# Attention-stage stores issued from GpSimd's queue, and a three-buffer ring for streamed weights

## The chip, the cores and the metric

The kernel runs on one core of one Trainium2 chip. The core has five engines that follow separate instruction streams: TensorE (PE in the profile, with its weight loads as PEld), VectorE (DVE), ScalarE (ACT), GpSimd (POOL) and SyncE (SP), which here only issues DMA transfers. Data lives in SBUF (on-chip, 128 partitions), matmul results in PSUM, everything else in HBM. The metric is device time in microseconds of one execution. The kernel before took 1733.87 us (median of three runs, 1732.55 to 1734.95).

## The reference, cut to what matters

One decoder block on 1024 tokens of width 1024, in float32. A normalised input `h` is projected by one wide weight; the parts are queries, keys and values of 24 heads in three groups (dilation 1, 4 and 16, window of 128 steps each), a gated convolution branch, and two gates. The three groups of a head slot are merged with their softmax denominators as weights.

```python
h = rms_norm(x, g_pre_mix)
q, k, v, glu_in, z_ga, z_gc = split(h @ w_in)
for g, (window, dilation) in enumerate(((128, 1), (512, 4), (2048, 16))):
    o_g, lse_g = dilated_group_attention(q[g], k[g], v[g], bias_tab[g], window, dilation)
alpha = softmax(stack(lses))                      # over the three groups
y_attn = sum_g(alpha[g] * outs[g]) @ w_attn_out
y_conv = silu(layer_norm(depthwise_conv31(u * sigmoid(gate)))) @ w_conv_out + b
merged = sigmoid(z_ga) * y_attn + sigmoid(z_gc) * y_conv
x = x + rms_norm(merged @ w_mix_out, g_post_mix)
x = x + rms_norm(swiglu(rms_norm(x, g_pre_ffn)), g_post_ffn)
```

## The kernel before, in words

Every large product is made from values split in two float32r parts, a high one and the rest, so one product is three matmuls (L321 to L323, or L305 to L309, or L940 to L944 for the values). The order of all work is written out by hand in one Python program; each engine executes its instructions in that order, and an instruction waits for the data and for the buffer that it needs.

**Buffers.** Most tiles are 128x1024 float32 and come from one pool, `slot()`, tag "b", of NSLOT = 43. `ring()`, tag "d", has NRING = 2 of the same size; it holds the attention outputs `O` of groups 0 and 1 and the residual rows `x2` of the mixing stage. `half()`, tag "c", has 11 of 128x512. A new tile takes the buffer that was released longest ago, and its first writer waits for the last user of that buffer.

**Stages, in order of time.** (1) The start and the plain projections, to about 111 us. (2) Twenty-three *pairs* to about 550 us: two weight tiles, "row1" and "row2", make one 2x2 block product in the manner of Winograd, seven products of 12 matmuls (`winograd`, `prod`). For the next pair SP loads the two raw tiles (`load_ahead`, L177), ACT makes the high parts (L195, L231), GpSimd the rest (L196, L232) and the sums of quarters: `s12` (L215, L216) and `s34` (L222, L223), in `quarters`. ACT also copies PSUM results out (L335, L340, L345). Beside it VectorE computes the convolution (L684). (3) Values and attention, to about 875 us. `v()` computes the values of one group for four heads at a time, six calls; each call writes two 128x1024 tiles `x`, ACT copies the results in (L950, L952), and `out` stores each by two transfers (L927). `timed()` fixes when, within a call, the weights of the next call are loaded and split: 6 and 15 ticks after its start (a tick is six matmuls there). Between these matmuls runs `attention()`: 96 steps in 12 stacks of 8, a stack being one group and one pair of heads. A step takes scores (L1038, `att_s`), adds the bias tile (L1041, DVE; the tile is loaded at L477), exponentiates (L1051, ACT), transposes (L1074, ACT L1079 and DVE L1080 take the parts) and multiplies with the values (L1095, L1097), of which VectorE makes the output (L1102). Before a stack, SP loads its operands (L866, L867, L873) and its values (L903 to L908), and GpSimd splits the values (L917, `value_parts`) and copies query parts across partitions (L882, L883, `double`; eight casts per stack). At the end of a stack of group 0 or 1, `tokens_out` stores its statistics and its output (L1060 for group 0, one transfer; L1064 for group 1, two transfers). `merge` combines the groups of a pair of heads; for the first two pairs the result goes to HBM (L1165). (4) Gates, output projections, mixing, and the FFN, whose first product is again made of pairs (twenty), to 1727 us. VectorE, not GpSimd, makes the sums there.

**Queues.** All these stores and loads are issued by SP, in program order. A transfer that waits for its data, or for a buffer, holds all transfers behind it in that queue.

Of the kernel before, what the change touches and what calls it, by code (L numbers as in the profile page):

```python
# [43 lines left out]
PLAIN = 2  # L44

LAST = 5
NSLOT = 43

NRING = 2
NHALF = 11  # L50


# [6 lines left out]
def f(ap):  # L59
    return ap.bitcast(F32)  # L60


class Build:
# [16 lines left out]
    def slot(self, dt=F32, shape=None):  # L80
        self.uid += 1
        return self.pool.tile(shape or [128, 1024], dt, tag="b", bufs=NSLOT, name=f"b{self.uid}")

    def ring(self):
        self.uid += 1
        return self.pool.tile([128, 1024], F32, tag="d", bufs=NRING, name=f"d{self.uid}")

# [84 lines left out]
    def load_ahead(self, i):  # L172
        while self.sent < min(len(self.jobs), i + 1):
            j = self.sent
            src, n, _ = self.jobs[j]
            self.raw[j] = self.slot()
            self.nc.sync.dma_start(self.raw[j][:, :n], src)  # L177
            self.sent += 1

# [19 lines left out]
    def quarters(self, i, c):  # L199


        nc = self.nc
        if c == 0:
            self.hl[i] = {}
        o = self.hl[i]
        r1, r2 = self.raw[i - 1], self.raw[i]
        a11, a12, a21, a22 = r1[:, :H], r1[:, H:], r2[:, :H], r2[:, H:]
        add = self.wsplit.tensor_tensor
        l, r = slice(0, H), slice(H, 2 * H)
        if c == 0:  # L210
            h, w = self.both(r1)
            o["A11"], o["A12"] = (h[:, l], w[:, l]), (h[:, r], w[:, r])
        elif c == 1:
            self.s12 = self.slot()
            add(self.s12[:, l], a21, a22, op=OP.add)  # L215
            add(self.s12[:, r], self.s12[:, l], a11, op=OP.add)  # L216
        elif c == 2:
            h, w = self.both(self.s12)
            o["S1"], o["S2"] = (h[:, l], w[:, l]), (h[:, r], w[:, r])
        elif c == 3:  # L220
            self.s34 = self.slot()
            add(self.s34[:, l], a11, a21, op=OP.add)  # L222
            add(self.s34[:, r], self.s12[:, r], a12, op=OP.add)  # L223
            self.s12 = None
        elif c == 4:
            h, w = self.both(self.s34)
            o["S3"], o["S4"] = (h[:, l], w[:, l]), (h[:, r], w[:, r])
            self.s34 = None
        else:
            x = self.slot(F32R)  # L230
            nc.scalar.copy(x[:, l], a22)  # L231
            add(x[:, r], a22, f(x[:, l]), op=OP.subtract)  # L232
            o["A22"] = (x[:, l], x[:, r])
            del self.raw[i], self.raw[i - 1], self.hl[i]
# [90 lines left out]

    def winograd(self, W, T, f11, f12, f21, f22):

# [5 lines left out]
        x1, x2, v1 = self.half(), self.half(), self.half()  # L333
        self.prod(X, W["A11"], T["B11"], True, False)
        nc.scalar.copy(x1, X)  # L335
        self.prod(Z, W["A12"], T["B21"], True, True)
        rest = f11(Z, x1)
        Z = x1 = None
        self.prod(X, W["S2"], T["T2"], False, False)
        nc.scalar.copy(x2, X)  # L340
        V = self.bank()
        if rest:
            rest()
        self.prod(V, W["S1"], T["T1"], True, False)
        nc.scalar.copy(v1, V)  # L345
        if self.sums:
            self.finish(self.sums)
            self.sums = None
            self.summed()
        self.prod(X, W["S3"], T["T3"], False, False)  # L350
        rest = f22(X, v1)
# [374 lines left out]
    def glu_pair(self, j, job):  # L726
# [12 lines left out]
        def f22(x, v):  # L739
            nc.vector.scalar_tensor_tensor(v, x, self.nbu[:, j:j + 1], v, op0=OP.add, op1=OP.add)  # L740
            s[1] = v
# [178 lines left out]
    def v(self, g, hg, now, then):  # L920

        nc = self.nc
        W = self.timed(now, then, 6, 15)

        def out(i, x):
            for e in range(2):
                nc.sync.dma_start(self.d_v[g, 2 * hg + e].rearrange("(t p) c -> p t c", p=128)[:, i - 2:i + 2],  # L927
                                  x.rearrange("p (t e c) -> p t e c", t=4, e=2)[:, :, e])
            self.vn += i == 6

        for i in range(0, 8, 2):
            ps = self.bank()
            for e in range(2):
                t = slice((i + e) * 128, (i + e + 1) * 128)
                o = ps[:, e * 256:(e + 1) * 256]
                for kt in range(KT):
                    hi, lo = W[kt // 4]
                    s = slice((kt % 4) * 256, (kt % 4 + 1) * 256)
                    a, b = self.hH[kt][:, t], self.hL[kt][:, t]
                    nc.tensor.matmul(o, a, hi[:, s], start=kt == 0, stop=False)  # L940
                    self.beat()
                    nc.tensor.matmul(o, a, lo[:, s], start=False, stop=False)  # L942
                    self.beat()
                    nc.tensor.matmul(o, b, hi[:, s], start=False, stop=kt == KT - 1)  # L944
                    self.beat()
                    if kt % 2:
                        self.tick()
            if i % 4 == 0:
                x = self.slot()
                nc.scalar.copy(x[:, :H], ps)  # L950
            else:
                nc.scalar.copy(x[:, H:], ps)  # L952
                self.later(2, lambda i=i, x=x: out(i, x))
                x = None
# [101 lines left out]
    def tokens_out(self, g, dst, src):  # L1056

        if g == 0:
            d = dst.rearrange("(u p) e -> p u e", p=128)
            self.nc.sync.dma_start(d, src)  # L1060
        else:
            d = dst.rearrange("(b p c) e -> b p c e", b=2, c=4)
            for b in range(2):
                self.nc.sync.dma_start(d[b], src[:, b::2, :])  # L1064

    def att_t(self, a):

# [43 lines left out]
    def merge(self, hp, st, last):  # L1111


        nc = self.nc

        late = 1 + (hp > 1)
        while hp > 1 and (self.fine is not None or hp > len(self.OT) + 2):
            yield 0
        O = [*self.others(hp), last]
        last = None  # L1120
        yield 1 + late
        t = self.tiny(96, "mrg", 2)
        m, r = (t[:, i * 16:(i + 1) * 16].rearrange("p (u e) -> p u e", u=8) for i in range(2))
        w = t[:, 48:].rearrange("p (g u e) -> p g u e", g=3, u=8)
        low, tot = st[:, :, :, 0:2], st[:, :, :, 2:4]
        nc.vector.tensor_reduce(m, low.rearrange("p g u e -> p u e g"), AX.X, OP.min)
        nc.vector.tensor_tensor(w, low, m.unsqueeze(1).to_broadcast([128, 3, 8, 2]), op=OP.subtract)
        nc.scalar.activation(t[:, 48:], t[:, 48:], AF.Exp, scale=-1.0)
        yield late
        nc.vector.tensor_tensor(tot, tot, w, op=OP.mult)  # L1130
        nc.vector.tensor_reduce(m, tot.rearrange("p g u e -> p u e g"), AX.X, OP.add)
        nc.vector.reciprocal(r, m)
        nc.vector.tensor_tensor(w, w, r.unsqueeze(1).to_broadcast([128, 3, 8, 2]), op=OP.mult)
        for g in range(3):
            y = O[g].rearrange("p (u h c) -> p u h c", u=8, h=2)
            a = w[:, g].unsqueeze(3).to_broadcast([128, 8, 2, 64])
            nc.vector.tensor_tensor(y, y, a, op=OP.mult)
            yield late
        nc.vector.tensor_tensor(O[1], O[1], O[2], op=OP.add)
        O[2] = y = a = None  # L1140
        yield late
        nc.vector.tensor_tensor(O[0], O[0], O[1], op=OP.add)
        O[1] = None
        yield 2 + 2 * late
        if hp < 2:
            hi = self.slot()
        else:
            hi, lo = self.slot(F32R), self.slot(F32R)
        for h in range(2):
            ps = self.bank("t")  # L1150
            for i in range(4):
                u = h * 4 + i
                nc.tensor.transpose(ps[:, i * 128:(i + 1) * 128], O[0][:, u * 128:(u + 1) * 128], self.ident)
            y = ps.rearrange("p (u m) -> p u m", u=4)
            a = hi.rearrange("p (m u) -> p u m", u=8)[:, h * 4:h * 4 + 4]
            nc.scalar.copy(a, y)
            if hp > 1:
                nc.vector.tensor_tensor(lo.rearrange("p (m u) -> p u m", u=8)[:, h * 4:h * 4 + 4], y, f(a),
                                        op=OP.subtract)
            ps = y = a = None  # L1160
            yield late
        if hp > 1:
            self.OT[hp] = hi, lo
        else:
            self.nc.sync.dma_start(self.d_ot[hp], hi)  # L1165

    def out_parts(self):

# [790 lines left out]
```

## Time and profile before

| what | before |
|---|---|
| median of three runs | 1733.87 us |
| the profiled execution | 1728.74 us |
| its span, first to last instruction | 1726.9 us |
| PE busy | 1703.5 us, 99% |
| DVE, ACT, POOL busy | 1237.1, 793.7, 462.5 us |
| granted TensorE clock | 0.999 |
| stores that the change moves (L927, L1060, L1064, L1165) | 24 + 8 + 16 + 2 transfers |

The profiled execution lies 1.8 us above its span, and 5.1 us below the median. Lines of the profile name an instruction by its source line; `x<-y` is output from input by tile name, and what stands in brackets after an instruction, or after a bar, is the idle time of its engine before it and what ended that time. "SPq" is SP's issuing queue; "b", "c" and "d" are the three kinds of buffers.

### The profile page before, as it was taken

What the parts mean: (1) busy time and instruction counts of PE and PEld (TensorE: products, weight loads), DVE (VectorE), ACT (ScalarE), POOL (GpSimd) and SP (SyncE); (2) the same over time, 40 slices, a digit from 0 to 9 for tenths busy, and PEclk for the clock granted to TensorE, in tenths of its full rate; (3) what the DMA queues carried; (4) which work ended last, traced back from release to release, by engine and by line L of the source; (5) the groups of instructions that cost most, each with busy time, mean ns of one, the idle gap of its engine ahead of it and who ended that gap; (6) DMA issues with size and microseconds to landing.
All of it is one profiled execution on the core that took longest, in us unless ns stands there. A gap on an engine that the chain in (4) does not pass through costs nothing.

```text
span 1726.9 us, 24514 instructions
## 1 busy us (share of the span) xinstructions
PE 1703.5 (99%) x8698; PEld 1448.2 (84%) x8698; DVE 1237.1 (72%) x2217; ACT 793.7 (46%) x1552; POOL 462.5 (27%) x337
## 2 busy tenths in 40 slices
PE   8999999999999999999999999999999999999998
PEld 7778888887888999999788888888888888888886
DVE  6879988789998576687664855676556555677686
ACT  6344343434444486667622346643333333454453
POOL 0017777787786043443300120000000000000000
PEclk9999999999999999999999999999999999999999
DMA  4342344345667898988945732223322322395334
GB/s 164 125 160 86 110 160 133 135 159 184 206 164 194 246 257 200 245 227 213 310 145 187 275 107 93 83 73 112 126 92 92 112 108 92 137 363 159 107 126 153
DMA packets 185398, 277.03 MB, mean 160 GB/s; under 512 B 55185, under 2 KB 106892, under 8 KB 185276
## 3 DMA queue, kind: packets, MB, share of 16 engines
q1 hardware_dynamic: 184876, 274.97, 50.2%
q8 instruction: 68, 1.11, 0.3%
q14 instruction: 54, 0.44, 0.1%
q10 hardware_dynamic: 288, 0.27, 0.0%
q0 software_dynamic: 112, 0.24, 0.0%
HBM read 184.81 MB, written 95.33 MB: 162 GB/s over the span
## 4 chain that ended last, share of the span: by engine, by line
PE 86%; POOL 5%; DVE 3%; DMA 3%; ACT 2%; issue 2%; SPq 0%; DVEq 0%; POOLq 0%; ACTq 0%
PE p L321 13%; PE p L322 13%; PE p L323 13%; PE p L1843 12%; PE p L1572 5%; PE p L305 5%; PE p L307 5%; PE p L309 5%; PE p L942 2%; PE p L940 2%; PE p L944 2%; POOL b L196 2%; PE p L554 2%; PE p L1038 2%; PE p L1074 2%
## 5 line engine op out<-in xcount | busy, mean ns | idle before, releaser
L321 PE MATMUL p<-b,b 128*128 128x512 f32 x1204 | 469.4, 390 | 3.7 <-ACT c L335 2.4
L323 PE MATMUL p<-b,b 128*128 128x512 f32 x1204 | 468.8, 389 | 0.2 <-POOL b L196 0.2
L322 PE MATMUL p<-b,b 128*128 128x512 f32 x1204 | 468.5, 389 | 0.0
L321 PEld LDWEIGHTS p<-b,b 128*128 128x128 f32 x1204 | 226.0, 188 | 53.7 <-ACT c L335 3.2
L323 PEld LDWEIGHTS p<-b,b 128*128 128x128 f32 x1204 | 226.0, 188 | 48.5 <-POOL b L196 1.3
L322 PEld LDWEIGHTS p<-b,b 128*128 128x128 f32 x1204 | 226.0, 188 | 46.4
L195 ACT CAST b<-b 128x1024 fp32r<-128x1024 f32 x131 | 137.8, 1052 | 178.4 <-DVE b L216 50.9
L1843 PE MATMUL p<-b,b 128*128 128x512 f32 x924 | 209.6, 389 | 0.0
L1843 PEld LDWEIGHTS p<-b,b 128*128 128x128 f32 x924 | 173.4, 188 | 36.0
L196 POOL TENSOR_TENSOR b<-b,b 128x1024 fp32r<-128x1024 f32 x66 | 158.8, 2406 | 116.3 <-ACT b L195 108.1
L196 DVE TENSOR_TENSOR b<-b,b 128x1024 fp32r<-128x1024 f32 x65 | 79.5, 1222 | 128.9 <-ACT b L195 128.9
L684 DVE SCALAR_TENSOR_TENSOR p<-b,par,p 128x511 f32<-128x511 f32 (+14 forms) x232 | 163.4, 738 | 0.0
L305 PE MATMUL p<-b,b 128*128 128x512 f32 x368 | 147.6, 401 | 0.0
L309 PE MATMUL p<-b,b 128*128 128x512 f32 x368 | 146.2, 397 | 0.0
L307 PE MATMUL p<-b,b 128*128 128x512 f32 x368 | 146.1, 397 | 0.0
L940 PE MATMUL p<-b,b 128*128 128x256 f32 x384 | 115.3, 300 | 0.0
L942 PE MATMUL p<-b,b 128*128 128x256 f32 x384 | 114.6, 298 | 0.0
L944 PE MATMUL p<-b,b 128*128 128x256 f32 x384 | 114.5, 298 | 0.0
L1180 DVE TENSOR_TENSOR b<-c,b 128x512 fp32r<-128x512 f32 x101 | 69.9, 693 | 46.9 <-ACT b L1179 46.6
L1179 ACT CAST b<-c 128x512 fp32r<-128x512 f32 x101 | 62.4, 618 | 63.8 <-DMA c<-dqA 19.8
L1179 ACT CAST b<-b 128x512 fp32r<-128x512 f32 x117 | 72.4, 619 | 40.6 <-DVE b L387 13.7
L1180 DVE TENSOR_TENSOR b<-b,b 128x512 fp32r<-128x512 f32 x117 | 80.3, 690 | 14.8 <-ACT b L1179 13.1
(226 smaller groups left out, 2994.1 us busy)
## 6 DMA issues: line engine op xcount, KB each, us to landing
b<-w_in SPq DMA_DIRECT2D x53, 512.0 KB, 5.7
b<-w_fi SPq DMA_DIRECT2D x44, 512.0 KB, 4.9
dk<-c SPq DMA_DIRECT2D x48, 256.0 KB, 5.7
dq<-c SPq DMA_DIRECT2D x48, 256.0 KB, 4.3
b<-dq SPq DMA_DIRECT2D x48, 256.0 KB, 8.9
b<-dk SPq DMA_DIRECT2D x48, 256.0 KB, 7.3
dqS<-c SPq DMA_DIRECT2D x44, 256.0 KB, 2.1
b<-w_fo SPq DMA_DIRECT2D x44, 256.0 KB, 5.3
```

Of the source, the lines that this page charges most:

```text
L196: self.wsplit.tensor_tensor(lo, x, f(hi), op=OP.subtract)
L305: nc.tensor.matmul(ps, hi[:, s], a, start=kt == 0, stop=False)
L307: nc.tensor.matmul(ps, hi[:, s], b, start=False, stop=False)
L309: nc.tensor.matmul(ps, lo[:, s], a, start=False, stop=kt == nk - 1)
L321: nc.tensor.matmul(ps, hi[:, s], a, start=first and kt == 0, stop=False, skip_group_check=True)
L322: nc.tensor.matmul(ps, hi[:, s], b, start=False, stop=False, skip_group_check=True)
L323: nc.tensor.matmul(ps, lo[:, s], a, start=False, stop=kt == 3, skip_group_check=True)
L684: nc.vector.scalar_tensor_tensor(A[i][:, j:], src[i][:, :H - j], w[i], A[i][:, j:], op0=OP.mult, op1=OP.add)
L940: nc.tensor.matmul(o, a, hi[:, s], start=kt == 0, stop=False)
L942: nc.tensor.matmul(o, a, lo[:, s], start=False, stop=False)
L1180: nc.vector.tensor_tensor(s[:, 512:512 + n], src, f(s[:, :n]), op=OP.subtract)
L1843: nc.tensor.matmul(acc[t], x, y, start=first and e == 0, stop=last and e == 2, skip_group_check=True)
```

## The change

Four edits. The stores of the values, of the attention outputs, of the statistics and of the first two merged heads are issued by GpSimd's queue and not by SP's. The ring grows from two buffers to three and the pool shrinks from 43 to 42, so the number of large buffers is the same. The raw row1 tiles, `s12` and the value tiles `x` come from the ring and no longer from the pool. In `v()` the next weights are loaded at tick 4 (6 before) and queued for splitting at tick 16 (15 before).

```diff
-NSLOT = 43
-NRING = 2
+NSLOT = 42
+NRING = 3
@@ load_ahead
-            src, n, _ = self.jobs[j]
-            self.raw[j] = self.slot()
+            src, n, kind = self.jobs[j]
+            self.raw[j] = self.ring() if kind == "row1" else self.slot()
@@ quarters
-            self.s12 = self.slot()
+            self.s12 = self.ring()
@@ v
-        W = self.timed(now, then, 6, 15)
+        W = self.timed(now, then, 4, 16)
...
-                nc.sync.dma_start(self.d_v[g, 2 * hg + e]...
+                nc.gpsimd.dma_start(self.d_v[g, 2 * hg + e]...
...
-                x = self.slot()
+                x = self.ring()
@@ tokens_out
-            self.nc.sync.dma_start(d, src)
+            self.nc.gpsimd.dma_start(d, src)
...
-                self.nc.sync.dma_start(d[b], src[:, b::2, :])
+                self.nc.gpsimd.dma_start(d[b], src[:, b::2, :])
@@ merge
-            self.nc.sync.dma_start(self.d_ot[hp], hi)
+            self.nc.gpsimd.dma_start(self.d_ot[hp], hi)
```

More of the change, by code (lines that the diff above doesn't have):

```diff
@@ L922, in v @@
         nc = self.nc
-        W = self.timed(now, then, 6, 15)
+        W = self.timed(now, then, 4, 16)
         def out(i, x):
             for e in range(2):
-                nc.sync.dma_start(self.d_v[g, 2 * hg + e].rearrange("(t p) c -> p t c", p=128)[:, i - 2:i + 2],
+                nc.gpsimd.dma_start(self.d_v[g, 2 * hg + e].rearrange("(t p) c -> p t c", p=128)[:, i - 2:i + 2],
                                   x.rearrange("p (t e c) -> p t e c", t=4, e=2)[:, :, e])
```

## The prediction

> **What bounds the kernel now.** I read the page's first lines, then the waits of TensorE, then the busy times by stage, and only then the queues of SP and POOL around each stall. Matmuls fill the span; only 23.4 us of it are free, and of these the change can touch at most what lies between start and end.
>
> ```profile
> span 1726.9 us, 24514 instructions
> ...
> PE 1703.5 (99%) x8698; PEld 1448.2 (84%) x8698; DVE 1237.1 (72%) x2217; ACT 793.7 (46%) x1552; POOL 462.5 (27%) x337
> ```
>
> The waits of PE (engine, line, releaser: us in total, times, longest) say which idle time there is. The first row is the start, which no edit touches.
>
> ```profile
> PE p L554 <- ACT b L530: 6.0, 1, 6.0
> PE p L1097 <- DVE c L1080: 3.7, 5, 1.2
> PE p L321 <- ACT c L335: 2.4, 2, 2.0
> PE p L1038 <- DVE stat L1041: 1.3, 1, 1.3
> ```
>
> By stage (busy us of PE, PEld, DVE, ACT, POOL in brackets with counts, then clock, DMA share, GB/s): the early pairs are full, the later pairs lose a little, and the values and attention lose 4.9 us. The granted clock is 1.00 in all three, so nothing is to be had from it.
>
> ```profile
> 125.00:350.00 225.00, 225.00 (x995) 186.29 (x994) 197.60 (x285) 89.40 (x133) 174.80 (x101) 1.00 0.36 120
> 350.00:550.00 200.00, 198.52 (x866) 161.64 (x865) 178.32 (x234) 84.53 (x126) 158.01 (x89) 1.00 0.61 180
> 572.00:847.00 275.00, 270.15 (x2252) 265.05 (x2251) 193.95 (x591) 184.08 (x532) 99.67 (x118) 1.00 0.88 233
> ```
>
> So this is a change worth a few microseconds either way: gains are bounded by the stalls, losses are not.
>
> **The change part by part.**
>
> *Term 1, the first pair (ring for s12 and row1).* ACT, DVE and PEld in order of time:
>
> ```profile
> 111.88 0.62 ACT L1179 CAST b<-b 128x512 fp32r<-128x512 f32 x1 [4.01 <-PE p L309]
> ...
> 118.62 0.60 ACT L335 COPY c<-p 128x512 f32<-128x512 f32 x1
> ...
> 111.66 0.69 DVE L215 TENSOR_TENSOR b<-b 128x512 f32<-128x512 f32 x1 [3.06 <-PE p L307]
> ...
> 119.27 0.19 PEld L321 LDWEIGHTS p<-b,b 128*128 128x128 f32 x1 [2.41 <-ACT c L335]
> ```
>
> DVE's s12 and ACT's high part each wait for a slot that a matmul still reads (3.06 and 4.01 us). The copy L335 comes behind them on ACT at 118.62, and PE stands still for 2.0 us (the wait row above). With s12 in the ring DVE need not wait, and with row1 and s12 out of the pool two tiles leave it against one slot taken away, so ACT's buffer is an older one. Three microseconds earlier, L335 is in time. Ends: 0 if ACT's slot is as late as now, 2.0 if both waits go. I take 2.0, since both have their releaser named.
>
> *Term 2, the pairs.* SP's queue waits longest in the whole program for a buffer that GpSimd releases; PEld's waits in these pairs are three groups:
>
> ```profile
> SPq L177 <- POOL b L223: 142.7, 22, 10.5
> ...
> PEld p L321 <- ACT c L340: 2.3, 3, 1.0
> PEld p L321 <- DVE c L838: 1.5, 3, 0.5
> PEld p L323 <- POOL b L196: 1.3, 3, 0.6
> ```
>
> Every load of a next row1 sits behind the sum L223 in 22 of 23 pairs, 6.5 us on average, with the stores of the pair behind it. In a ring of three, with two tiles per pair in the order row1, s12, a new row1 takes the buffer of an s12 that was done one pair earlier, so this wait goes. But who is late next? The largest stalls look like this:
>
> ```profile
> 430.46 0.62 ACT L231 CAST b<-b 128x512 fp32r<-128x512 f32 x1 [2.52 <-POOL b L196]
> 430.99 0.58 ACT L340 COPY c<-p 128x512 f32<-128x512 f32 x1
> ...
> 431.62 0.19 PEld L321 LDWEIGHTS p<-b,b 128*128 128x128 f32 x1 [0.71 <-ACT c L340]
> ```
>
> ACT's L231 waits for the slot of s34, which L196 has just read, and the copy L340 waits behind it. At that point of a pair the old s12 is dead already and the new row1 is the only tile that has left the pool, against the one slot taken away: the number of free slots is unchanged, and this wait stays. POOL (158.01 of 200 us busy) and DVE are as loaded as before. The three groups sum to 5.1 us; ends 0 and 5.1; I take 1.0, for the stores that are no longer held and for a weight that arrives earlier.
>
> *Term 3, weights of the values.* SP and ACT:
>
> ```profile
> 612.93 1.18 SPq L177 DMA_DIRECT2D b<-w_v  x1
> ...
> 620.03 0.62 ACT L188 CAST b<-b 128x512 fp32r<-128x512 f32 x1 [1.56 <-DMA b<-w_v]
> ```
>
> The stall of 1.3 us in the wait row of L1038 follows this: ACT stands for w_v, and the first exponentials and DVE's parts come after it. Two ticks earlier are 12 matmuls of 275/2252 = 0.122 us, 1.5 us, and the two value stores in front of this load leave SP. The split one tick later (0.7 us) goes the other way. Ends -0.7 and 1.3; I take 0.6.
>
> *Term 4, the bias tiles at the end of attention.* SP's queue, then DVE and PEld:
>
> ```profile
> SPq L873 <- DMA dv<-b: 5.0, 2, 4.2
> ...
> 822.26 1.08 SPq L873 DMA_DIRECT2D b<-dk  x2
> 823.45 2.16 SPq L1064 DMA_DIRECT2D datt<-d  x2
> 825.65 0.63 SPq L908 DMA_DIRECT2D b<-dv  x1
> 826.37 0.39 SPq L477 DMA_DIRECT2D c<-rep  x1
> ...
> 832.33 0.29 DVE L1041 CUSTOM_DVE_ANT_0 c<-p,c 128x128 f32<-128x128 f32 x1 [3.56 <-DMA c<-rep]
> ...
> 855.34 0.29 DVE L1041 CUSTOM_DVE_ANT_0 c<-p,c 128x128 f32<-128x128 f32 x1 [1.32 <-DMA c<-rep]
> ...
> 833.49 0.19 PEld L1097 LDWEIGHTS p<-b,c 128*128 128x128 f32 x1 [1.46 <-DVE c L1080]
> ...
> 856.25 0.19 PEld L1097 LDWEIGHTS p<-b,c 128*128 128x128 f32 x1 [1.47 <-DVE c L1080]
> ```
>
> The bias tile is issued behind an operand load that waits 4.2 us for the slot of a value tile still being stored, and behind two output stores (2.16 us). Both leave: 4.2 + 2.2 = 6.4 us, against a DVE wait of 3.56. What can hold it instead is L908, which must wait until its values have been stored. PE would get back 1.46 and 1.47, 2.9 us; ends 0 and 2.9; I take 1.9.
>
> *Term 5, fifty stores on GpSimd.* The only transfers that GpSimd issues now are three at the start; the rows also show the landing times of a store from SP and of one transfer from GpSimd, and a stack's casts:
>
> ```profile
> L426 POOL DMA_DIRECT2D ident<-p_ident x1 | 0.7, 682 | 0.8 <-POOLq L1951 0.8
> L429 POOL DMA_DIRECT2D tab<-p_tab x1 | 0.5, 517 | 0.0
> ...
> dv<-b SPq DMA_DIRECT2D x24, 256.0 KB, 6.3
> ...
> par<-p_par POOLq DMA_DIRECT2D x1, 164.0 KB, 6.1
> ...
> 670.56 0.38 SPq L1060 DMA_DIRECT2D datt<-d  x1
> ...
> 668.47 0.60 POOL L882 CAST b<-b 64x512 fp32r<-64x512 f32 x1
> ...
> 673.16 0.61 POOL L883 CAST b<-b 64x512 fp32r<-64x512 f32 x1
> ...
> 680.47 0.53 PEld L1038 LDWEIGHTS p<-b,b 128*128 128x128 f32 x4
> ...
> L882 POOL CAST b<-b x48: 604/610/1493, 603.7 to 845.0; 64x512 fp32r<-64x512 f32 x48
> ```
>
> 128 rows cost 682 ns, 32 rows 517 ns: 1.7 ns a row. A store of 512 pieces (values, group 1) is then about 1.3 us, of 1024 pieces (group 0) 2.2 us; if all of the 682 ns grew with the rows, 2.7 and 5.5. Sum: 24 x 1.3 for values, 2 x (4 x 2.2 + 8 transfers x 1.3) for outputs and statistics, 2 x 0.7 for merged heads, 71 us, or at the upper end 24 x 2.7 + 2 x (4 x 5.5 + 8 x 2.7) + 1.4 = 153. POOL is busy 99.7 of 275 us there, so even that fits. What counts is the order: an output store waits for the last L1102 of its stack, and behind it on POOL stand the eight casts for the next stack. They run from 668.47 to 673.77 now, 5.3 us, and that stack starts at 680.47. Afterwards they start when the store is issued, 670.56 + 2.2, and end at 678.1, still 2.4 us ahead. A value store waits for ACT's copy, with the split of the next values (L917) behind it, needed four steps later. Ends 0 and, by the next part, a slipping start of eight stacks. I take a loss of 1.0.
>
> The smaller pool elsewhere (FFN output, gates): buffers run ahead of PE there by several steps, so one slot less only shortens the lead. I cost it at nothing; without that cover it is one wait like that of term 1, 2 to 4 us. The merged heads (two transfers) are read back only in the output stage; nothing.
>
> Sum: -2.0 - 1.0 - 0.6 - 1.9 + 1.0 = -4.5 us against the profiled 1728.74 us, which is 5.1 us below the median of the runs; on the median, 1733.87 - 4.5 = **1729.4 us**.
>
> **Rivals.** *Hidden anyway.* SP's waits are long, but SP is not on PE's path; if ACT and POOL keep their own loop in the pairs (term 2 at 0), the bias tile now waits behind L908, and only term 1 comes, less term 5, the time is 1732.9. For it: the early pairs lose nothing (225.00 of 225.00) although SP waits there as well. Against: terms 1 and 4 name stalls of PE itself.
>
> *POOL becomes late (slower).* If a pair of output stores takes longer than 680.47 - 670.56 - 2.7 (the first four casts, which the first half of a stack needs) = 7.2 us, the next stack starts late, and PE follows. Pieces at the upper price, 2 x 2.7 = 5.4 us, do not reach this; stretched as the longest cast is (1493/610 = 2.4) they take 13 us and cost 5.9 us in each of eight stacks. At 9 us it is 1.8 x 8 = 14, so 1733.87 - 4.5 + 14 = 1743. Against: the median cast is 610 ns, so most are not stretched. [...]
>
> *A pool that is too small (slower).* Where the ring does not help, at the start's second normalisation and in the output stages, one wait like ACT's 4.01 us reaches PE, and term 1 is lost too: 1733.87 + 4.0 - 1.0 + 1.0 = 1738.
>
> **How the numbers follow.** Forecast 0.50, hidden 0.28, POOL late 0.12, pool too small 0.10. Since 0.2% is 3.5 us, about what a measurement tells here, the first is faster, the second the same, the others slower. The forecast's own range runs from all upper ends of terms 1 to 4 with term 5 at 0, -11.3, of which I expect no more than three quarters, 1725, to 1731. The range reaches to the hidden case and the small pool, 1725 to 1738, and leaves POOL late out.
>
> **What would show it.** Term 1: no PE wait for L335 near 119 us. Term 2: SP's wait for L223 gone, PE's waits for L340 still there. Term 3: no ACT wait for w_v near 620. Term 4: no DVE wait for the bias tile. Term 5: store instructions on POOL of 1 to 2.5 us, and casts that end before their stack. The prediction is wrong if the stores take over 3 us each on POOL, if L1038 then waits for L882 or L883, or if L340 loses its wait in every pair and the pairs give all 5.1 us.

## The result, and the profile after

The changed kernel takes 1727.03 us (median, 1724.21 to 1730.45), against 1732.17 us for the kernel before on the same chip: a ratio of 0.9973, 95% interval 0.9962 to 0.9983, or -5.1 us. Forecast were 1729.4 us and -4.5 us. The profiled execution took 1728.2 us, 1.2 above its own median, while that of before (1728.74) lay 3.4 below the median of its runs. So the two spans differ by only 0.5 us, and where the time goes is read here stage by stage and not from the spans.

The head of the page, and the waits of TensorE (engine, line, releaser: us in total, times, longest) of the changed kernel:

```profile
span 1726.4 us, 24521 instructions
...
PE 1705.3 (99%) x8698; PEld 1453.6 (84%) x8698; DVE 1234.4 (71%) x2217; ACT 793.6 (46%) x1552; POOL 497.1 (29%) x387
```

```profile
PE p L554 <- ACT b L530: 6.0, 1, 6.0
PE p L1038 <- DMA b<-dk: 4.2, 3, 2.4
PE p L1097 <- DVE c L1080: 2.1, 4, 0.7
...
PE p L321 <- ACT c L340: 0.3, 1, 0.3
```

The wait for L335 is gone, that for `L1041` too, and that for `L1080` fell from 3.7 to 2.1. A new one stands second: scores (L1038) that wait for operands still on their way, 4.2 us where it was 0.2 before. The same three stages as in the prediction, in the same columns (us; PE, PEld, DVE, ACT, POOL busy; clock, DMA share, GB/s):

```profile
125.00:350.00 225.00, 225.00 (x994) 186.48 (x994) 197.76 (x287) 89.75 (x133) 175.53 (x102) 1.00 0.39 129
350.00:550.00 200.00, 199.73 (x880) 164.79 (x879) 179.19 (x235) 86.06 (x127) 159.02 (x90) 1.00 0.60 177
572.00:847.00 275.00, 270.51 (x2228) 265.47 (x2226) 184.99 (x585) 180.77 (x530) 128.56 (x161) 0.99 0.81 227
```

The pairs lose 0.27 us of idle time instead of 1.48. The values and attention lose as much as before, 4.5 against 4.9, have 29 us more of work on POOL, and the clock is 0.99 and no longer 1.00. Two fixed points of the program make this comparable between kernels: the first weight load of L1204 that follows a gap (the pairs are over) and the one of L1313, in the mixing stage. Attention's last multiplication (L1097) comes 180.1 us ahead of this second point in every kernel here, so a difference between the two points arises in values and attention. Each row gives the start of the load first; here before, then after:

```profile
559.97 0.19 PEld L1204 LDWEIGHTS p<-b,ones 128*128 128x128 f32 x1 [0.24 <-issue]
...
1057.43 0.42 PEld L1313 LDWEIGHTS p<-ident,b 128*128 128x128 f32 x4 [0.64 <-ACT b L1319]
```

```profile
556.78 0.19 PEld L1204 LDWEIGHTS p<-b,ones 128*128 128x128 f32 x1 [0.24 <-issue]
...
1057.93 0.42 PEld L1313 LDWEIGHTS p<-ident,b 128*128 128x128 f32 x4 [0.64 <-ACT b L1319]
```

The pairs end 3.2 us earlier. From there to the second point the kernel before needed 1057.43 - 559.97 = 497.5 us and the changed one 1057.93 - 556.78 = 501.2, which is 3.7 **longer**. So the profile says that the change gains in the pairs and gives back in attention, although the stores, the ticks and the value tile all act there.

### The profile page after: what moved, and what is told of

Read it like the earlier page. It is cut to its first block, busy times and chain, and to the rows that moved or that the text cites. A ratio compares the mean times of both kernels' runs of the same rounds, so it can differ in the third digit from the quotient of the medians.

```text
span 1726.4 us, 24521 instructions
## 1 busy us (share of the span) xinstructions
PE 1705.3 (99%) x8698; PEld 1453.6 (84%) x8698; DVE 1234.4 (71%) x2217; ACT 793.6 (46%) x1552; POOL 497.1 (29%) x387
## 4 chain that ended last, share of the span: by engine, by line
PE 92%; DMA 3%; DVE 1%; ACT 1%; issue 1%; POOL 1%; SPq 0%; DVEq 0%; ACTq 0%; POOLq 0%
PE p L321 15%; PE p L322 15%; PE p L323 15%; PE p L1843 12%; PE p L1572 5%; PE p L305 5%; PE p L309 5%; PE p L307 5%; PE p L942 2%; PE p L944 2%; PE p L940 2%; PE p L1038 2%; PE p L1074 1%; DMA b<-dk 1%; PE p L1097 1%; PE p L1095 1%
## 5 line engine op out<-in xcount | busy, mean ns | idle before, releaser
L321 PE MATMUL p<-b,b 128*128 128x512 f32 x1204 | 469.2, 390 | 0.3 <-ACT c L340 0.3
L322 PE MATMUL p<-b,b 128*128 128x512 f32 x1204 | 469.0, 390 | 0.0
L323 PE MATMUL p<-b,b 128*128 128x512 f32 x1204 | 468.9, 389 | 0.0
L321 PEld LDWEIGHTS p<-b,b 128*128 128x128 f32 x1204 | 226.1, 188 | 47.8 <-ACT c L340 0.7
L1843 PE MATMUL p<-b,b 128*128 128x512 f32 x924 | 209.6, 389 | 0.0
L305 PE MATMUL p<-b,b 128*128 128x512 f32 x368 | 147.7, 401 | 0.0
L309 PE MATMUL p<-b,b 128*128 128x512 f32 x368 | 146.4, 398 | 0.0
L307 PE MATMUL p<-b,b 128*128 128x512 f32 x368 | 146.2, 397 | 0.0
L195 ACT CAST b<-d 128x1024 fp32r<-128x1024 f32 x86 | 90.4, 1051 | 105.1 <-POOL d L216 55.1
L196 POOL TENSOR_TENSOR b<-d,b 128x1024 fp32r<-128x1024 f32 x44 | 106.8, 2428 | 79.8 <-ACT b L195 72.4
L196 DVE TENSOR_TENSOR b<-d,b 128x1024 fp32r<-128x1024 f32 x42 | 51.3, 1221 | 101.0 <-ACT b L195 101.0
L1572 PE MATMUL p<-b,b 128*128 128x512 f32 x384 | 89.4, 392 | 0.0
```

The costliest lines, as they stand in the source:

```text
L196: self.wsplit.tensor_tensor(lo, x, f(hi), op=OP.subtract)
L305: nc.tensor.matmul(ps, hi[:, s], a, start=kt == 0, stop=False)
L307: nc.tensor.matmul(ps, hi[:, s], b, start=False, stop=False)
L309: nc.tensor.matmul(ps, lo[:, s], a, start=False, stop=kt == nk - 1)
L321: nc.tensor.matmul(ps, hi[:, s], a, start=first and kt == 0, stop=False, skip_group_check=True)
L322: nc.tensor.matmul(ps, hi[:, s], b, start=False, stop=False, skip_group_check=True)
```

## The experiments

The four edits were taken apart into three parts: *buffers* (ring of three, pool of 42, row1, `s12` and the value tile in the ring), *stores* (the fifty transfers on GpSimd) and *ticks* (4 and 16 for 6 and 15). In the table, "pairs end" is the first of the two points just shown and "attention" the time from it to the second, both in the profiled execution.

| kernel | ratio to before, 95% interval | pairs end | attention |
|---|---|---|---|
| before | 1 | 559.97 | 497.5 |
| after (all three parts) | 0.9973 [0.9962, 0.9983] | 556.78 | 501.2 |
| buffers | 0.9959 [0.9947, 0.9971] | 555.08 | 497.7 |
| stores | 1.0062 [1.0048, 1.0076] | 562.58 | 507.9 |
| ticks | 1.0018 [1.0006, 1.0029] | 562.27 | 500.6 |
| buffers, ticks | 0.9984 [0.9972, 0.9997] | 554.48 | 506.4 |
| buffers, stores | 0.9957 [0.9940, 0.9974] | 555.46 | 500.5 |
| buffers, output stores | 0.9942 [0.9925, 0.9958] | 554.99 | 495.5 |
| the same, ticks | 0.9937 [0.9923, 0.9950] | 554.95 | 499.5 |
| the same, bias tiles on GpSimd | 0.9952 [0.9937, 0.9967] | 554.53 | 501.9 |
| the same, bias tiles on ACT | 0.9955 [0.9943, 0.9968] | 555.48 | 500.7 |
| buffers, bias tile first | 0.9966 [0.9954, 0.9978] | 555.09 | 500.9 |
| buffers, stores, bias tile first | 1.0000 [0.9989, 1.0011] | 555.22 | 503.7 |
| stores, value tile in the ring | 1.0231 [1.0217, 1.0245] | 595.56 | 499.2 |

**Buffers alone.**

```diff
-NSLOT = 43
-NRING = 2
+NSLOT = 42
+NRING = 3
...
+            self.raw[j] = self.ring() if kind == "row1" else self.slot()
...
+            self.s12 = self.ring()
...
+                x = self.ring()
```

> Only the buffers change: pool 42, ring 3, with row1, s12 and the value tiles in the ring; all stores stay on SP, loads and splits of the value weights at ticks 6 and 15. Ring theory: the stalls that went are those of the pairs (2.4 us near 119 us, 4.0 of 5.1 us between 353 and 515 us), so this kernel alone is 5 to 7 us faster than the kernel before, ratio 0.996 to 0.997, and has no wait of L1038 for L883. Queue theory: the gain comes from SP's queue being free of the stores; then this kernel lies within 2 us of the kernel before.

Measured: 1723.51 us, 0.9959 of before. One part of the change gives more than the whole: 0.0041 x 1733 = 7.1 us, and L1038 never waits for L883, as the ring theory had it. The weight loads of TensorE that waited between 100 and 550 us are down to two; in before there was a gap of 2.41 us at 119 and nine more of 5.1 us together:

```profile
428.27 0.19 PEld L321 LDWEIGHTS p<-b,b 128*128 128x128 f32 x1 [0.71 <-ACT c L340]
...
491.09 0.19 PEld L321 LDWEIGHTS p<-b,b 128*128 128x128 f32 x1 [0.38 <-DVE c L838]
```

Its span is 5.4 us shorter than before's, of which 4.9 are there at the end of the pairs. The stage of attention is as long as before (497.7 and 497.5), so the buffers act in the pairs and hardly anywhere else.

**Stores alone.**

```diff
-                nc.sync.dma_start(self.d_v[g, 2 * hg + e]...
+                nc.gpsimd.dma_start(self.d_v[g, 2 * hg + e]...
...
-            self.nc.sync.dma_start(d, src)
+            self.nc.gpsimd.dma_start(d, src)
```

> Only the fifty stores move to GpSimd's queue; pool 43, ring 2, ticks 6 and 15. Ring theory: the pairs keep their stalls (2.4 and 5.1 us), and the stores cost or give at most 3 us, ratio 0.998 to 1.002. Queue theory: 4 to 5 us faster, ratio 0.997, with the waits of DVE for the bias tiles gone.

Measured: 1742.45 us, 1.0062, slower than either theory allowed. Two new waits in attention make the loss, one of VectorE and one of ScalarE (rows: start, length, instruction, idle time before it and what ended it):

```profile
740.69 0.42 DVE L1102 TENSOR_REDUCE b<-p 128x128 f32<-128x256 f32 x1 [5.75 <-DMA dv<-b]
```

```profile
831.85 0.62 ACT L916 CAST b<-b 128x512 fp32r<-128x512 f32 x1 [8.26 <-DMA dv<-b]
```

```profile
741.23 0.19 PEld L1095 LDWEIGHTS p<-b,c 128*128 128x128 f32 x1 [3.49 <-issue]
...
833.57 0.29 PEld L1095 LDWEIGHTS p<-b,c 128*128 128x128 f32 x1 [6.48 <-issue]
```

"DMA dv<-b" is a value store that still reads a pool slot: L1102 and L916 have been given the slot of a value tile, and TensorE then stands for 3.5 and 6.5 us. In before a wait for such a slot is seen on SP's queue only (L866, L867 and L873, the last being the 5.0 us of term 4); here it is met by the engines that compute. The same trace also has the stall at 120 us, which the stores don't touch.

**Stores with only the value tile in the ring.** This tests that reading.

```diff
 (the stores as above)
-NSLOT = 43
-NRING = 2
+NSLOT = 42
+NRING = 3
...
-                x = self.slot()
+                x = self.ring()
```

> The stores on GpSimd and three ring buffers, but of the three tiles only the value tile lies in the ring; row1 and s12 stay in the pool, which has 42 slots instead of 43. The stores alone gave 1.0062, with 9.3 us of waits of TensorE for what follows L1102 and L1095 in attention. Cover theory (those waits come from pool slots that a value store still reads): they go with the value tile out of the pool, the stalls of the pairs (2.4 and 5.1 us) stay or grow a little with the slot taken away: 0.998 to 1.002, and no wait for dv<-b. Queue theory (the loss comes from the casts behind the stores on GpSimd, whatever the tiles): 1.004 to 1.008, with L1095's stalls still there.

Measured: 1771.64 us, 1.0231. The expectation was wrong by some 40 us, and in the other stage. In attention the reading held: no wait for "dv<-b" is left, and the stage takes 499.2 us where the stores alone took 507.9. But the pairs end 35.6 us later than in before. The waits of the weight loads say why:

```profile
PEld p L321 <- ACT c L340: 28.2, 17, 2.1
PEld p L323 <- POOL b L196: 8.5, 10, 0.9
```

In before these two rows were 2.3 us in 3 waits and 1.3 us in 3. Row1 and `s12` are in the pool again and the pool has one slot fewer; a single slot of 43 makes nearly every pair stall, even the early ones, where before had none. So the pool of before is just large enough for its pairs, and taking a slot away costs nothing in the pairs of the changed kernel only since two tiles per pair leave the pool at the same time.

**Ticks alone.**

```diff
-        W = self.timed(now, then, 6, 15)
+        W = self.timed(now, then, 4, 16)
```

> Only the ticks change, 4 and 16 in place of 6 and 15. Both theories: within 1 us of the kernel before, ratio 0.9995 to 1.0005; ACT's wait for w_v near 620 us is shorter by up to 1.5 us. A third theory, that this shift moves the start of attention against the loads of the second stack, expects 3 us or more in one direction and a changed wait of L1038.

Measured: 1734.88 us, 1.0018. The stall of 1.5 us at 621 is gone, as term 3 has it, and the kernel is slower all the same: new gaps of 0.7 us at 637 (L1038 for L882) and of 2.1 at 860 with the clock at 0.66 in 860 to 865. The ring and the queue theory had both expected less than 1 us; 0.0018 x 1733 = 3.1 us is what the third allowed.

**Buffers and ticks.**

> The changed kernel with its stores left on SP. Ring theory: at least as fast as the changed kernel, 5 to 8 us faster than the kernel before (ratio 0.9955 to 0.997), since the stalls for L883 near 631 us and the half clock behind them belong to the stores or to the earlier start of attention. Queue theory: no faster than the kernel before by more than 2 us.

Measured: 1730.39 us, 0.9984, slower than the buffers alone by 0.0025 x 1733 = 4.3 us, and the intervals don't overlap. The ring theory had expected 0.9955 to 0.997 and missed; that the gain over before is 2 us at most, as the queue theory had it, lies within the interval. In attention the longest gap is 4.7 us at 836, behind bias tiles for which VectorE waits 12.6 us in three waits (4.9 in two in before).

**Buffers and stores**, the whole change without the ticks:

> The three buffers of their own and the stores on GpSimd, with the value weights at their old place (6, 15). The buffers alone gave 0.9959 of before, the stores alone 1.0062, all three edits 0.9973. Cover theory (the stores alone lost 10.7 us because in that kernel a value tile keeps its pool slot until its store has landed, and DVE's L1102 and ACT's L916 waited 5.8 and 8.3 us for such slots; with value tiles in the ring this loss cannot happen): no wait for dv<-b, and the stores cost between -2 and +1 us on top of the buffers, so 0.995 to 0.9965 of before. Queue theory (a store on GpSimd costs whatever the buffers are, since the casts L882 and L883 stand behind it): PE waits for L883 again as in the changed kernel, 2 us, and the ratio is that of the changed kernel or worse, 0.997 to 1.001. If the ratio is near 0.995 the earlier value weights are what made the changed kernel slower than the buffers alone.

Measured: 1724.77 us, 0.9957, against 0.9959 for the buffers alone: on top of the buffers the stores cost nothing that can be told, and no wait for "dv<-b" occurs. What the cover theory had not expected is that TensorE waits for L883 all the same, 2.1 us near 631, as in the changed kernel; in this trace the clock is 0.50 from 634 to 639 behind it, and attention takes 500.5 us where it took 497.7 with the buffers alone. The large loss of the stores alone belonged to the slots, then. A value store does stand in front of casts and waits for ScalarE's copy, here in the changed kernel:

```profile
605.80 1.52 POOL L927 DMA_DIRECT2D dv<-d  x2 [7.83 <-ACT d L952]
607.36 3.52 POOL L882 CAST b<-b 64x512 fp32r<-64x512 f32 x1
```

With the buffers alone the casts of the first stack are over by then. This store does no harm: the first scores follow the end of the pairs after 614.34 - 555.46 = 58.9 us with the stores and 613.97 - 555.08 = 58.9 without them.

**Buffers and output stores**, the value stores left on SP:

```diff
 (buffers as above; tokens_out and merge on GpSimd)
                 nc.sync.dma_start(self.d_v[g, 2 * hg + e]...
```

> The buffers, and on GpSimd only the stores of attention outputs, statistics and merged heads (26); the 24 value stores stay on SP. Against the kernel with the buffers alone (0.9959) this takes 2.2 us of output stores, and later 2.3 us of statistics, from SP in front of the bias tiles and operands. Queue theory: DVE's wait for the bias tile near 825 us gets shorter by about 2 us and TensorE's stall of 2.25 us goes: 0.994 to 0.9955. If the stores of outputs hurt through the casts behind them on GpSimd, a wait of L1038 for L882 or L883 comes in and the ratio is 0.997 or more.

Measured: 1720.78 us, 0.9942, the lower end of what was expected, and with the next one the best kernel here, 0.0031 x 1733 = 5.4 us below the changed one. Attention takes 495.5 us, less than in any other. The wait for L883 near 631 is gone, while the stall of 0.85 us at 616 that all stores together had removed is back: TensorE arrives later at the second stack, whose casts start at the same time (623.94, with all stores 624.33). The stall of 1.40 us at 828 for the bias tile is shorter than with the buffers alone (2.25), and the one at 852 is gone, as the queue theory has it.

The interval overlaps with those of the buffers alone and of all stores, so that each of these two steps is a gain isn't certain; attention is 2.2 and 5.0 us shorter in the traces.

**The same with ticks 4 and 16.**

> The buffers and the output stores on GpSimd (0.9942), with the value weights at ticks 4 and 16 as in the change. Given the buffers alone the ticks cost 4 us (0.9984 against 0.9959), given buffers and all stores 2.8 us (0.9973 against 0.9957). If the ticks cost by themselves, because attention comes earlier against the loads of its second stack and its bias tiles, 0.9955 to 0.998, with stalls near 630 and 835 us. If they only cost where the value or output stores are late, 0.993 to 0.9945, with the stall of 0.85 us at 616 gone.

Measured: 1720.99 us, 0.9937: no difference from 0.9942. The stall of 0.85 us at 616 is gone, and one of 0.8 us at 631 for L882 has come. So the ticks are worth nothing here: 4.3 us lost beside the stores on SP, 0.0016 x 1733 = 2.8 us beside all stores on GpSimd (0.9973 against 0.9957, intervals that overlap), none beside output stores on GpSimd. Why it depends on the stores isn't shown.

**Where a bias tile waits.** In the best kernel the bias tile for the stack at 828 us was issued at 815.61, and VectorE had it at 827.02:

```profile
815.61 0.47 SPq L477 DMA_DIRECT2D c<-rep  x1
```

```profile
827.02 0.29 DVE L1041 CUSTOM_DVE_ANT_0 c<-p,c 128x128 f32<-128x128 f32 x1 [3.68 <-DMA c<-rep]
```

That is 11.4 us from issue to use, with a median landing of the twelve tiles of 6.9 here and 5.4 in before. Four kernels tried to have it earlier, in three ways: from GpSimd's queue, from ScalarE's, and ahead of the two `dk` tiles.

```diff
-        nc.sync.dma_start(bt.rearrange("p (h c) -> p h c", h=2),
+        nc.gpsimd.dma_start(bt.rearrange("p (h c) -> p h c", h=2),
```

> The buffers and the output stores on GpSimd (0.9942 of before), and the twelve bias tiles L477 issued from GpSimd as well. In the kernel without this, the bias tile of the stack at 828 us was issued at 815.6 and DVE waited for it until 827.0, 11.4 us after its issue where the median of twelve is 5.4, so it is late in landing and not in issue. Queue theory: it lands late since operand loads stand ahead of it in SP's queue; from GpSimd's queue it lands in 5 to 7 us, DVE's wait of 3.7 us and the stall of 1.4 us with its 0.66 clock go: 0.9915 to 0.993. Traffic theory: all transfers share the engines (DMA share 0.91 in this stretch), it lands as late: 0.994 to 0.9955, and the issue of 0.7 to 0.9 us ahead of the casts gives no gain.

> The same with the twelve bias tiles issued from ScalarE's queue, where no other transfer is issued. By the queue theory the bias tile lands in 5 to 7 us here too, but ScalarE, which holds the copies and exponentials of attention, issues it: 0.992 to 0.9945. By the traffic theory 0.994 to 0.9965.

Measured: 0.9952 and 0.9955, with intervals that overlap that of the best kernel (0.9942). In both VectorE no longer waits for the bias tile, and TensorE waits for something else. With GpSimd's queue, the weight loads, then TensorE's waits:

```profile
825.77 0.37 PEld L1038 LDWEIGHTS p<-b,b 128*128 128x128 f32 x2 [2.58 <-issue]
...
848.91 0.31 PEld L1038 LDWEIGHTS p<-b,b 128*128 128x128 f32 x2 [1.95 <-issue]
```

```profile
PE p L1038 <- DMA b<-dk: 4.3, 2, 2.5
```

The bias tile came in time and the `dk` operands were late instead; with ScalarE's queue TensorE stands 2.9 us at 849, also for L1038. The bias tile of the stack at 828 us landed 9.5 us after its issue from GpSimd's queue (at 813.9), 9.0 from ScalarE's (at 815.3) and 10.3 from SP's (at 815.61); the medians of the twelve are 6.2 from GpSimd's and 9.0 from ScalarE's. So an issuing queue without other transfers, as ScalarE's is in this stage, did not make this transfer fast. This is the traffic theory, and both ratios are those it gave: with a DMA share of 0.86 to 0.91 (790 to 850 us in these three kernels), a transfer that a stack needs was late in each of the three, the bias tile with SP's queue and another one with the other two.

```diff
         elif i < 4:
+            if i == 2:
+                p[3] = self.bias_tile(p[0], p[1])
             k = self.slot(F32R)
...
-        else:
-            p[3] = self.bias_tile(p[0], p[1])
```

> The buffers, all stores on SP, and the bias tile of a stack issued ahead of its two dk tiles instead of behind them. It is meant to measure what the late bias tile costs by itself: in the kernel with the buffers alone TensorE waits 2.25 us at 829 and 1.52 us at 852 for what follows L1041's wait for that tile, and the granted clock is 0.66 for 5 us after the first, another 1.7 us. If the bias tile is the cause, both stalls and the drop go, -3 to -5.5 us against the buffers alone: 0.993 to 0.9945. If the dk tiles are then late by as much, L1038 waits for dk instead and the ratio stays at 0.995 to 0.997.

> The buffers, the stores on GpSimd and the earlier bias tile. If the two ways to an earlier bias tile act on the same stall, this is as fast as the faster of them and no faster, 0.993 to 0.995 of before; if they add up, 0.991 to 0.993.

Measured: 0.9966 and 1.0000, against 0.9959 and 0.9957 without this edit. For the first the intervals overlap; the second is slower by 0.0043 x 1733 = 7.5 us. The stalls at 829 and 852 did go. In the first kernel one of 3.7 us came at 841, where ScalarE waits for a tile of the gates (`dact`) and everything of attention behind it:

```profile
839.63 0.62 ACT L1179 CAST b<-c 128x512 fp32r<-128x512 f32 x1 [4.48 <-DMA c<-dact]
```

In the second there were 1.4 and 1.6 us at 631 and 633, behind operands of the second stack, and 3.1 at 847. The ratio of the first was among those expected, its cause was not; the second was slower than either case foresaw, and its profiled execution was the shortest of twelve (1729.19, median 1732.56), so its trace shows only part of that. Once more a load that came earlier made another one late.

## Why the prediction was right, and where it was not

The time was right, 1729.4 forecast and 1727.0 measured, but only because the errors of its terms cancel, and that they cancel is luck.

**Term 1 was right** (-2.0 forecast; the gap of 2.41 us is gone).

**Term 2 was too small**: -1.0 forecast, and of the nine gaps of 5.1 us two of 1.1 are left, -4.0. The failing step is the one sentence that the wait of L231 for L196's slot stays, taken as an answer for all three groups. That wait stays to the hundredth, and L340's gap behind it nearly so (0.69 us for 0.71):

```profile
428.77 0.62 ACT L231 CAST b<-b 128x512 fp32r<-128x512 f32 x1 [2.52 <-POOL b L196]
```

But it is one of nine. Of the others (three for L838, three for L196, two more for L340) only one for L838 is left, of 0.38 us; the step had looked at one gap only. SP's wait for L223 (142.7 us) is gone but for 0.9 us, as forecast. That this had anything to do with the gain isn't shown; the kernel with one slot less says that the number of free slots decides there.

**Term 3 was wrong**: -0.6 forecast. The wait for `w_v` went and the stall of 1.5 us at 621 with it, but the term didn't ask what is late next. It is the second stack, whose casts wait for their operands until 625.28 in this kernel, and until 624.15 with the buffers alone, however early TensorE comes:

```profile
625.28 0.61 POOL L882 CAST b<-b 64x512 fp32r<-64x512 f32 x1 [7.92 <-DMA b<-dq]
```

```profile
630.99 0.31 PEld L1038 LDWEIGHTS p<-b,b 128*128 128x128 f32 x2 [0.49 <-POOL b L883]
632.86 0.37 PEld L1038 LDWEIGHTS p<-b,b 128*128 128x128 f32 x2 [1.56 <-POOL b L883]
```

So 1.5 us went and 2.05 came. The ticks alone don't make this wait: with the buffers, all stores and the old ticks it is 2.1 us too, and with the old ticks and the output stores alone it is absent. That L1038 would wait for L882 or L883 stands among the prediction's own signs of being wrong, and it came true.

**Term 4 was wrong**: -1.9 forecast. The bias tile is issued earlier, as forecast (821.68 instead of 826.37), and is used no earlier (832.22 instead of 832.33):

```profile
821.68 0.39 SPq L477 DMA_DIRECT2D c<-rep  x1
```

```profile
832.22 0.29 DVE L1041 CUSTOM_DVE_ANT_0 c<-p,c 128x128 f32<-128x128 f32 x1 [3.09 <-DMA c<-rep]
```

The step that sets the 6.4 us which leave SP against a wait of 3.56 took the time of issue for the time of landing: the time from issue to use grew from 6.0 to 10.5 us. The DMA engines were full in both kernels (share 1.07 before and 0.99 after, from 815 to 840 us); which transfers this tile shared them with isn't shown. TensorE's gaps of 1.46 and 1.47 became 0.99 and 0.37, and one of 0.34 at 851 became 2.55 at 853, behind `dk`: +0.6 for these three, where -1.9 was forecast.

**Term 5** (+1.0): the instructions were forecast nearly twice as long as they are, and the place was not the one named. A store instruction takes (rows: tile, count, then total us and mean ns, then idle time before it and what ended it)

```profile
L927 POOL DMA_DIRECT2D dv<-d x24 | 18.1, 760 | 47.2 <-ACT d L952 47.2
L1064 POOL DMA_DIRECT2D datt<-d x8 | 5.7, 716 | 5.8 <-DVE stat L1041 3.3 <-DVE d L1102 2.2
L1060 POOL DMA_DIRECT2D datt<-d x4 | 3.7, 918 | 9.8 <-DVE d L1102 9.8
```

and all fifty 38 us (18.1 + 5.7 + 5.7 + 3.7 + 3.6 + 1.2), not 71. By the prediction's own counts, 512 pieces for L1064 and 1024 for L1060, a piece more costs (918 - 716) / 512 = 0.4 ns and not 1.7. The 24 value stores lie between 750 and 792 ns, beside a VectorE that is busy two thirds of the time (184.99 of 275 us), those of L1064 between 709 and 746, those of L1060 between 894 and 935. None is stretched by anything like the 2.4 that the rival "POOL becomes late" took from the longest cast, and this rival did not come about. The price was put on GpSimd's order of work, and there it is nothing that can be told (0.9957 with the stores against 0.9959), although GpSimd stands 47.2 us in 8 waits for ScalarE's copies. The real price, 10.7 us with the stores alone, comes from slots that are free later, and the ring spares it; the prediction had not seen that the stores need the ring.

**What no term had** is the clock, which the prediction took as 1.00 throughout. In the changed kernel it falls twice, after the new gaps at 33 and at 631 to 633 us (columns: us; PE busy and count; clock, DMA share, GB/s):

```profile
36.00:40.00 4.00, 4.00 (x12) 0.57 0.01 2
...
634.00:641.00 7.00, 7.00 (x36) 0.54 1.04 233
```

By estimate from these clocks the falls cost 4 x 0.43 + 7 x 0.46 = 4.9 us, more than the gaps themselves (0.9 and 2.05). The second of these, 3.2 us, is most of the 3.7 by which attention became longer. The first lies at the start, where no edit acts, and two kernels with the same program up to attention don't have it: with the buffers and the stores there is no such gap, and the pairs end 1.3 us earlier (555.46); with the buffers and the output stores the clock is 1.00 from 34 to 40 us. It belongs to this one execution and not to the change.

In sum terms 1 and 2 gave 6.4 us of gaps where 3.0 were forecast, and terms 3 to 5 with the clock took some of it back where 1.5 were to come on top. How much was taken back in the median can't be read from one execution, and no other execution of before has a trace. Two kernels that differ from before only behind the pairs (stores alone, ticks alone) get there 2.6 and 2.3 us later than before's profiled execution, and with the ticks alone the clock is 0.66 from 120 to 125 us, after the same stall. The mean granted clock, which is on record for every execution, points the same way. Before's profiled execution has 0.999. Of 20 executions of before on one chip, those at 0.998 and 0.999 took 1728.4 to 1730.8 us and those at 0.995 took 1735.3 to 1736.8; a mean of 0.997 for 0.999 is by estimate 0.002 x 1730 = 3.5 us, as much as the profile lies below the median. This fits a gain of 5.1 us between the medians and of 0.5 between the spans, since the changed kernel's profile (0.996) is like the middle of its own executions. Where in before's executions the clock fell is not shown.

## What to carry to other kernels

Before you move a store to another queue, ask which buffer it holds and who is given that buffer next: here engines waited 5.8 and 8.3 us for such a buffer, and a ring for the stored tiles took the whole loss away. A pool that is just large enough made one slot worth 36 us here, so a tile that leaves the pool was worth more than a queue that gets shorter. Where transfers filled the DMA engines, as here (a share of 0.86 to 0.91 from 790 to 850 us in three of these kernels), an earlier issue only changed which transfer was late, in all four kernels that tried it: read the landing and not the issue.

## What the hardware showed that was not expected

A stall of TensorE cost twice in some of these executions. In the same stretch and after the same stall of 2.41 us (L321 for L335), the clock was 1.00 in the profiled execution of before, and 0.66 over 5 us with the ticks alone, here in this order:

```profile
120.00:125.00 5.00, 5.00 (x24) 1.00 0.11 41
```

```profile
120.00:125.00 5.00, 4.99 (x15) 0.66 0.26 97
```

A stall of 1.4 us at 828 was followed by 0.66 over 5 us (1.7 us lost, by estimate) in the best kernel, while stalls of 1.5 us at 621 in before and of 2.55 at 853 in the changed kernel were followed by none (1.00 from 622 to 640 and from 853 to 865). With the stores alone, the stalls of 3.5 and 6.5 us were followed by one, 0.83 from 740 to 750 and 0.63 from 833 to 840. In attention in six kernels (before, after, the output stores with the ticks or with bias tiles on GpSimd or ACT, and the value tile alone in the ring), no gap of under 1.3 us that stood alone was followed by a clock below 1.00; at the start one of 0.9 us, that at 33 in the changed kernel, was followed by 0.57. The row of the best kernel:

```profile
830.00:835.00 5.00, 5.00 (x25) 0.66 0.73 197
```

Where a stretch lies within a fall, the clock is about half: 0.57 and 0.54 in the changed kernel, 0.50 with the buffers and all stores. The same stall of 2.41 us was followed by a fall in one execution and by none in another, so its length alone doesn't say whether the clock falls. What starts a fall isn't settled by these runs.
